# Copying out both upper parts of a PSUM bank before forming its two lower parts, in the second attention and in the stick-breaking mixer

## The chip, the cores and the metric

The kernel runs on one core of one Trainium2 chip. The metric is the device time of one execution in microseconds, taken as the median of several runs.

## The reference, cut to what matters

The program is a stack of two transformer-like blocks over 1024 tokens of width 1024, in f32: a differential attention and a multi-head latent attention (the first block), then a block with three mixers (spatial gating, stick-breaking, dilated window) and a gated feed-forward part. The change touches two places, the second attention and the stick-breaking mixer. In both a square of weights `p` (128 queries by up to 1024 keys) is multiplied with the values:

```python
# second attention (8 heads): all 1024 keys
p = jax.nn.softmax(sc, axis=-1)
return jnp.einsum('bhqk,bkhd->bqhd', p.astype(v.dtype), v)

# stick-breaking (6 heads): only the keys before the query
before = (k_pos[None, :] < q_pos[:, None])[None, None]
z = jnp.einsum('bqhd,bkhd->bhqk', q_blk, k).astype(jnp.float32) * scale
log_beta = jax.nn.log_sigmoid(z)
log_stay = jnp.where(before, jax.nn.log_sigmoid(-z), 0.0)
tail = lax.cumsum(log_stay, axis=3, reverse=True) - log_stay
weight = jnp.where(before, jnp.exp(log_beta + tail), 0.0)
return jnp.einsum('bhqk,bkhd->bqhd', weight.astype(v.dtype), v)
```

## The kernel before, in words

Nearly every product is made in three matmuls of a short f32 type (`fp32r`): each operand is split into an upper part (a cast, on ScalarE) and a lower part, which is the operand less its upper part (`lo`, a `tensor_sub`, by default on VectorE).

The program has four phases: the first attention (`layer0`, some 120 to 760 us in the trace), the second attention (`layer1`, its heads some 1050 to 1520 us), the mixers (the stick-breaking heads some 1790 to 2095 us) and the feed-forward part. The first attention's order on each engine is written out by hand in a table and pinned. In all other phases the order is not pinned: the functions are generators that are interleaved (`merge`, `pace`, `ahead`), and when the context is left a scheduler puts the instructions of each engine in order, by the program's order, by priorities (`tc.high_priority`) and by its own estimate of when each is ready; it also settles the buffers (`TileContext(nc, schedule_with_timeline_sim=True, auto_bufs=True)`). Each engine then runs its instructions strictly in that order.

In the second attention a tile is 128 queries of a head against 1024 keys. TensorE forms the scores (tile `s`), VectorE takes the row maximum, ScalarE the exponential (tile `e`), VectorE the reciprocal of the sum, GpSimd scales the row. Then `pt_fill` turns the row: four 128x128 transposes fill one PSUM bank (tile `m`, taken from `pm`), so that a tile has two banks. Each bank holds four key blocks, and is read out in two parts of two key blocks each (128x256): the upper part by ScalarE into one `pt` tile, the lower part by VectorE into the next. After four tiles `pv` multiplies `v` with the eight `pt` tiles. There are 8 heads of 8 tiles: 64 tiles and 128 banks.

In the stick-breaking mixer a tile has `qi + 1` key blocks, for `qi` from 0 to 7. A head then has 12 banks, of which 8 are read in two parts and 4 in one; six heads give 72 banks, 48 of them with two parts. The row passes VectorE (minimum), ScalarE (`Exp`, `Ln`), VectorE (a scan), ScalarE (`Exp`) and GpSimd (a product) before it is turned by the same `pt_fill`.

In the first attention the function `turns` of `da_tile` does the corresponding work, in PSUM tiles named `t`: there both upper parts are already copied first and the two lower parts are formed after them. The dilated-window mixer turns its rows with code of its own. Neither is touched.

A PSUM bank is one object to the framework's tracking of dependences: an instruction of one engine that reads a bank is made to wait for an earlier reader of the same bank on another engine.

Of the kernel before, what the change touches and what calls it, by code (L numbers as in the profile page):

```python
# [122 lines left out]
class Net:  # L123
# [689 lines left out]
    def pt_fill(self, pts, p, slot, ktiles):  # L813

        nc = self.nc
        qs = slice(slot * 128, slot * 128 + 128)
        for g in range((ktiles + 3) // 4):
            n = min(4, ktiles - 4 * g)
            ps = self.pm((128, 4, 128))
            for i in range(n):  # L820
                kt = 4 * g + i
                nc.tensor.transpose(ps[:, i], p[:, kt * 128:(kt + 1) * 128], self.ident)
            for i in range(0, n, 2):
                m = min(2, n - i)
                hi, lo = (pts[4 * g + i + x][:, 0:m, qs] for x in range(2))
                nc.scalar.copy(hi, ps[:, i:i + m])
                self.lo(lo, ps[:, i:i + m], hi)

    def pv(self, v, pts):

# [1330 lines left out]
```

## Time and profile before

| what | value |
|---|---|
| time, median of 3 runs | 2925.15 us (2916.08 to 2933.8) |
| the profiled execution's own time | 2909.92 us |
| its span | 2907.9 us |
| mean granted clock of TensorE | 0.956 |
| TensorE busy | 2629.5 us (90%) |
| VectorE busy | 2099.3 us (72%) |
| ScalarE busy | 1421.6 us (49%) |
| GpSimd busy | 1292.2 us (44%) |

The profile is that of one execution, which was a little faster than the median. Busy times are unions over the whole span; the stages differ, so that a change in one is to be read from that stage. In the views PE is TensorE's matmuls and PEld its weight loads, DVE is VectorE, ACT is ScalarE, POOL is GpSimd. All instructions of the kernel carry the line of one helper, so that groups are told apart by tile names.

### The profile page before, as it was taken

The numbers are of one execution on the slowest core, as the hardware profiler recorded it, in microseconds if no ns is written. First come the engines' busy times: TensorE is split into PE (matmuls) and PEld (weight loads), VectorE is DVE, ScalarE is ACT, GpSimd is POOL, SyncE is SP. The second block draws the span as 40 slices with busy tenths as digits, with TensorE's granted clock in tenths as the row PEclk, the third lists the DMA queues.
The fourth block names the chain that finished last, engine by engine and source line by source line (L and its number), as shares of the span: only waits on it lengthen the run. The fifth ranks groups of instructions, "written<-read, shape, count | busy, mean of one in ns | idle before, by whom it ended". The sixth has DMA issues, their size and how long they took to land. (4 is left out here: it accounts for less than half of the span.)

```text
span 2907.9 us, 34523 instructions
## 1 busy us (share of the span) xinstructions
PE 2629.5 (90%) x12023; PEld 2128.7 (73%) x12023; DVE 2099.3 (72%) x2696; ACT 1421.6 (49%) x2609; POOL 1292.2 (44%) x779
## 2 busy tenths in 40 slices
PE   7899999998899979999997798887978999997897
PEld 4678787887777867877775687776766777776676
DVE  7577877778642596667768563778768888899865
ACT  5455555556444534544554453667544344443432
POOL 2423323342344532212243332444447878778761
PEclk8999999999999999999998999999989999998998
DMA  7233333234541473223342356332621222234564
GB/s 292 66 97 101 109 109 105 66 95 141 174 131 42 127 254 106 71 89 118 117 132 80 80 82 112 91 87 85 197 89 51 88 79 73 87 124 146 187 237 147
DMA packets 308402, 338.91 MB, mean 117 GB/s; under 512 B 37428, under 2 KB 232068, under 8 KB 308228
## 3 DMA queue, kind: packets, MB, share of 16 engines
q1 hardware_dynamic: 308228, 336.69, 39.3%
q8 instruction: 96, 1.57, 0.2%
q14 instruction: 78, 0.64, 0.1%
HBM read 231.17 MB, written 60.89 MB: 100 GB/s over the span
## 5 line engine op out<-in xcount | busy, mean ns | idle before, releaser
L111 PE MATMUL m<-h,wh 128*128 128x512 f32 x3480 | 985.0, 402 | 48.1 <-DVE h L111 14.4
L111 PEld LDWEIGHTS m<-h,wh 128*128 128x128 f32 x3480 | 669.4, 194 | 204.2 <-DVE h L111 18.2
L111 POOL TENSOR_TENSOR wl<-wr,wh 128x1024 fp32r<-128x1024 f32 (+1 forms) x146 | 333.5, 2291 | 429.6 <-ACT wh L111 393.4
L111 PE MATMUL u<-h,wh 128*128 128x512 f32 x1264 | 408.3, 404 | 1.4 <-ACT h L111 0.8
L111 POOL TENSOR_SCALAR e<-e,cf 128x1024 f32<-128x1024 f32 x128 | 152.6, 1193 | 564.8 <-DVE cf L111 403.5
L111 PE MATMUL m<-h,wl 128*128 128x512 f32 x840 | 336.8, 402 | 7.8 <-POOL wl L111 7.8
L111 ACT ACTIVATE e<-s,cf 128x1024 f32<-128x1024 f32 x192 | 216.0, 1126 | 240.4 <-DVE cf L111 221.9
L111 ACT CAST wh<-wr 128x1024 fp32r<-128x1024 f32 (+3 forms) x252 | 202.6, 810 | 170.1 <-PE m L111 67.7
L111 DVE TENSOR_REDUCE cf<-s 128x1 f32<-128x1024 f32 x192 | 228.3, 1217 | 69.6 <-PE s L111 69.2
L111 PEld LDWEIGHTS u<-h,wh 128*128 128x128 f32 x1264 | 233.1, 191 | 47.5 <-ACT h L111 1.2
L111 PE MATMUL u<-h,wl 128*128 128x512 f32 x632 | 252.5, 400 | 12.7 <-POOL wl L111 12.7
L111 PE MATMUL s<-kk,qq 128*128 128x512 f32 (+3 forms) x752 | 187.3, 386 | 35.8 <-DVE e L111 18.7
L111 ACT CAST pt<-m 128x256 fp32r<-128x256 f32 (+2 forms) x396 | 140.1, 376 | 155.1 <-PE m L111 88.4
L111 PE MATMUL s<-h,wh 128*128 128x512 f32 x720 | 182.8, 399 | 35.5 <-DVE h L111 18.2
L111 PEld LDWEIGHTS m<-h,wl 128*128 128x128 f32 x840 | 164.1, 195 | 44.5 <-POOL wl L111 9.0
L111 DVE SCALAR_TENSOR_TENSOR e<-z,cf,e 128x1023 f32<-128x1023 f32 (+1 forms) x88 | 175.8, 2008 | 24.8 <-ACT e L111 24.6
L111 PE MATMUL s<-h,h 128*128 128x512 f32 x640 | 171.5, 414 | 20.8 <-DVE h L111 14.3
L111 PEld LDWEIGHTS s<-h,wh 128*128 128x128 f32 x720 | 136.5, 192 | 71.3 <-DVE h L111 19.7
L111 DVE TENSOR_TENSOR pt<-m,pt 128x256 fp32r<-128x256 f32 (+2 forms) x396 | 155.0, 416 | 41.6 <-ACT pt L111 34.6
L111 PEld LDWEIGHTS s<-kk,qq 128*128 128x128 f32 x752 | 135.9, 196 | 65.8 <-DVE e L111 20.4
L111 PE MATMUL m<-pt,v 128*128 128x512 f32 (+3 forms) x668 | 151.9, 371 | 17.1 <-ACT pt L111 8.6
L111 PEld LDWEIGHTS s<-h,h 128*128 128x128 f32 x640 | 122.3, 196 | 52.5 <-DVE h L111 17.8
(285 smaller groups left out, 4848.0 us busy)
## 6 DMA issues: line engine op xcount, KB each, us to landing
wr<-in_w_in_dram SPq DMA_DIRECT2D x61, 512.0 KB
wr<-in_w_out_dram SPq DMA_DIRECT2D x48, 512.0 KB
tb<-in_w_ada_dram SPq DMA_DIRECT2D x48, 512.0 KB
wr<-in_w_up_dram SPq DMA_DIRECT2D x47, 512.0 KB
qq<-ab SPq DMA_DIRECT2D x144, 128.0 KB
wr<-in_ada_w_dram SPq DMA_DIRECT2D x32, 512.0 KB
tf<-act SPq DMA_DIRECT2D x30, 512.0 KB
wr<-in_w_down_dram SPq DMA_DIRECT2D x30, 512.0 KB
```

What stands on the lines that cost most here:

```text
L111: ins = f(*args, **kw)
```

## The change

In `pt_fill` the loop over the two parts of a bank, which issued for each part the cast and then the subtraction, becomes two loops: first all casts of the bank, then all subtractions. Instructions, shapes and tiles stay the same. The function has two callers, `mla_attention` (second attention) and `mixer_b_attention` (stick-breaking).

```diff
@@ -820,11 +820,11 @@
             for i in range(n):
                 kt = 4 * g + i
                 nc.tensor.transpose(ps[:, i], p[:, kt * 128:(kt + 1) * 128], self.ident)
-            for i in range(0, n, 2):
-                m = min(2, n - i)
-                hi, lo = (pts[4 * g + i + x][:, 0:m, qs] for x in range(2))
-                nc.scalar.copy(hi, ps[:, i:i + m])
-                self.lo(lo, ps[:, i:i + m], hi)
+            parts = [(pts[4 * g + i], pts[4 * g + i + 1], i, min(2, n - i)) for i in range(0, n, 2)]
+            for hi, _, i, m in parts:
+                nc.scalar.copy(hi[:, 0:m, qs], ps[:, i:i + m])
+            for hi, lo, i, m in parts:
+                self.lo(lo[:, 0:m, qs], ps[:, i:i + m], hi[:, 0:m, qs])
```

## Rows read from the trace of the kernel before

**Rows 1.** The page: span, and busy time and share of each engine.
```profile
span 2907.9 us, 34523 instructions
...
PE 2629.5 (90%) x12023; PEld 2128.7 (73%) x12023; DVE 2099.3 (72%) x2696; ACT 1421.6 (49%) x2609; POOL 1292.2 (44%) x779
```

**Rows 2.** Busy time by stage: first attention, second attention, stick-breaking.
```profile
core 0: us, PE busy (x) PEld busy (x) DVE busy (x) ACT busy (x) POOL busy (x), PEclk, DMA share, GB/s
120.00:760.00 640.00, 611.61 (x2914) 497.07 (x2913) 506.88 (x717) 361.73 (x728) 214.62 (x118) 0.98 0.36 101
1050.00:1520.00 470.00, 443.06 (x2176) 364.26 (x2175) 327.62 (x618) 236.77 (x521) 121.23 (x102) 0.96 0.38 114
1790.00:2095.00 305.00, 260.47 (x1300) 216.33 (x1299) 228.25 (x318) 183.85 (x365) 130.15 (x76) 0.94 0.41 108
```

**Rows 3.** Groups by shape, whole span: busy us, mean ns; idle before, releasers.
```profile
L111 ACT CAST pt<-m 128x256 fp32r<-128x256 f32 x356 | 126.3, 374 | 146.5 <-PE m L111 80.1 <-DVE pt L111 61.1 <-issue 3.1
...
L111 DVE TENSOR_TENSOR pt<-m,pt 128x256 fp32r<-128x256 f32 x356 | 139.2, 415 | 35.1 <-ACT pt L111 31.5
L111 DVE TENSOR_TENSOR pt<-t,pt 128x256 fp32r<-128x256 f32 x256 | 95.8, 416 | 84.1 <-ACT pt L111 78.3 <-DMA qq<-ab 5.6
```

**Rows 4.** Timeline of ScalarE, one tile of the second attention.
```profile
1261.79 0.36 ACT L111 CAST pt<-m 128x256 fp32r<-128x256 f32 x1
1262.65 0.65 ACT L111 CAST pt<-m 128x256 fp32r<-128x256 f32 x2 [0.49 <-DVE pt L111]
...
1265.30 0.37 ACT L111 CAST pt<-m 128x256 fp32r<-128x256 f32 x1 [1.24 <-DVE pt L111]
```

**Rows 5.** Timeline of VectorE, the same tile.
```profile
1262.19 0.42 DVE L111 TENSOR_TENSOR pt<-m,pt 128x256 fp32r<-128x256 f32 x1
1263.12 0.42 DVE L111 TENSOR_TENSOR pt<-m,pt 128x256 fp32r<-128x256 f32 x1 [0.51 <-ACT pt L111]
1263.71 1.23 DVE L111 TENSOR_REDUCE cf<-s 128x1 f32<-128x1024 f32 x1 [0.16 <-PE s L111]
1264.86 0.41 DVE L111 TENSOR_TENSOR pt<-m,pt 128x256 fp32r<-128x256 f32 x1
...
1265.71 0.42 DVE L111 TENSOR_TENSOR pt<-m,pt 128x256 fp32r<-128x256 f32 x1 [0.38 <-ACT pt L111]
```

**Rows 6.** Timeline of one bank in the first attention.
```profile
404.63 0.65 ACT L111 CAST pt<-t 128x256 fp32r<-128x256 f32 x2 [4.90 <-PE t L111]
...
405.68 0.76 DVE L111 TENSOR_TENSOR pt<-t,pt 128x256 fp32r<-128x256 f32 x2 [5.56 <-DMA qq<-ab]
```

**Rows 7.** TensorE's waits, second attention: waited for; us, times, longest.
```profile
PE s L111 <- DVE h L111: 8.5, 3, 3.5
...
PE m L111 <- DVE v L111: 3.4, 1, 3.4
PE m L111 <- DVE t L111: 3.1, 2, 1.7
...
PE m L111 <- DVE cf L111: 2.4, 3, 1.2
PE m L111 <- DVE pt L111: 1.3, 2, 0.8
```

**Rows 8.** TensorE's waits, stick-breaking.
```profile
PE s L111 <- DVE e L111: 18.7, 13, 6.4
...
PE m L111 <- DVE pt L111: 4.5, 6, 1.6
PE m L111 <- DVE h L111: 3.0, 1, 3.0
...
PE m L111 <- ACT pt L111: 1.8, 3, 1.0
```

**Rows 9.** VectorE's subtractions by shape, second attention, then stick-breaking.
```profile
L111 DVE TENSOR_TENSOR pt<-m,pt 128x256 fp32r<-128x256 f32 x256 | 100.7, 417 | 29.4 <-ACT pt L111 26.0
...
L111 DVE TENSOR_TENSOR pt<-m,pt 128x256 fp32r<-128x256 f32 x97 | 37.3, 409 | 5.7 <-ACT pt L111 5.5
```

## The prediction

> **What bounds the kernel now.** I read the page first: TensorE is busy 90% of the span and nothing else is above 73% [rows 1]. That is an average, so I cut it into the stages where `pt_fill` runs. In the second attention TensorE is busy 443.06 of 470 us, which leaves 26.9 us idle; VectorE has 327.62 us of work there (70%), ScalarE 236.77 (50%). In the stick-breaking stretch TensorE is busy 260.47 of 305 us, 44.5 us idle, and VectorE 228.25 (75%) [rows 2]. So TensorE sets the pace in both, loosely in the second, and a change that gives it no work and takes none away can only act on these 71.4 us of idle time, or add to them.
>
> The third view, the groups by shape, says whether the order that the change removes costs anything at all. Before a cast out of an `m` bank ScalarE sat idle 61.1 us in total until a VectorE subtraction had ended; VectorE before its subtractions sat idle 31.5 us until a cast had ended [rows 3]. The timeline of one tile shows how: the second cast of a bank begins 0.04 us after the first subtraction has ended (1262.19 + 0.42 = 1262.61, then 1262.65). The same happens in the other bank, but there the first subtraction stands behind a 1.23 us row maximum on VectorE and ends at 1265.27, so the last cast starts only at 1265.30, after 1.24 us of idle time on ScalarE [rows 4, 5]. A part that lies ready in PSUM waits for a subtraction of another part.
>
> The fourth view, who TensorE waits for, says whether that reaches the bound. In the second attention only 1.3 us of its waits, twice, end on a subtraction into `pt`; in stick-breaking 4.5 us in six, and 1.8 us in three on a cast into `pt` [rows 7, 8]. Together 7.6 us: the big idle times on ScalarE lie almost wholly beside TensorE work.
>
> **The change part by part.** Nothing is added or dropped: no DMA, no matmul, no tile; 128 banks of the second attention and 48 of stick-breaking have two parts, 176 in all, and only they change. (24 more stick-breaking banks have one part, which stay as they are.) What is left out is the alternation: three handovers between engines in a bank become one.
>
> *One bank by itself.* Before, with nothing else in the queues: 0.36 + 0.42 + 0.37 + 0.42 with three handovers of 0.04 makes 1.69 us. After: two casts back to back took 0.65, one handover 0.04, two subtractions back to back 0.76 [rows 4 to 6], in sum 1.45 us. So a bank is free 0.24 us earlier, and its first lower part comes 0.29 us later (0.69 after the start in place of 0.40). Where another instruction slips in between the two subtractions, as the 1.23 us row maximum can, a bank gains over 1 us: in the tile shown, from the first cast to the last subtraction, 1261.79 to 1266.13, it is 4.34 us, and four casts and four subtractions without gaps would need about half of that.
>
> *On the engines.* ScalarE can lose most of its 61.1 us of waits; at 50% it is no bound, and what it does next is mostly waiting for something else anyway, so I cost this gain at nothing. Its cover is the TensorE work of other tiles and of the next head; without that cover it would be worth at most the 7.6 us above. VectorE saves about 0.08 us where two subtractions newly stand together (0.42 + 0.42 against 0.76), at most 176 x 0.08 = 14 us over 775 us of which it is idle 219: nothing on the path.
>
> *The one wait that grows.* The first subtraction needs only its own cast, but will now wait for both. The trace shows this where the order is already so: in the first attention two casts run from 404.63 to 405.28 and the pair of subtractions begins at 405.68 [rows 6]. Behind the waiting subtraction stand, in VectorE's queue, row maxima, scans, the minimum that frees a score bank, and the lower parts of the next head's keys; TensorE waits for those (`h`, `v`, `t`, `e` in [rows 7, 8]). Bounds for VectorE's new idle time: from below, one chance to wait in place of two, half of today's 31.5 us gone, about -16 us; from above, the rate of the first attention, 78.3 us over 128 banks, 0.61 us each, against 0.20 in the second attention (26.0 over 128) and 0.11 in stick-breaking (5.5 over 48) [rows 3, 9], which makes (0.61 - 0.20) x 128 = 52 us and (0.61 - 0.11) x 48 = 24 us more. I take the lower end's direction, since the casts that were held back 61.1 us will now run early and VectorE finds them done more often; the first attention's order was pinned by hand and is a farther row.
>
> The rows above show a second cast that waits although it reads other columns of the bank than the subtraction does [rows 4, 5]. The Trainium skill (PSUM — Partial Sum Buffer, section on PSUM bank collisions) says why: no two of TensorE, ScalarE and VectorE may be in one bank and quadrant at once, even reading disjoint columns, so such accesses have to be kept apart by semaphores. That rule speaks against the change as well: the first subtraction can't start beside the second cast. If a subtraction needed its own cast alone, each bank would gain 0.29 us on its first lower part; neither the sum nor the range uses this.
>
> *The order of everything else.* These two phases are not pinned. The scheduler sees 176 banks with other dependences and may place fills, weight casts and row maxima elsewhere in 775 us. No row prices that. It can't win more than the 71.4 us of TensorE's idle time in both stages [rows 2]; I take 0 with a quarter of it, 18 us, on either side.
>
> **The sum.** Second attention, half of 1.3: -0.6 us. Stick-breaking, about half of 4.5 + 1.8: -3.0. VectorE's 16 us fewer idle us reach TensorE in the share in which it waits for VectorE at all, 18.7 of 470 and some 26 of 305 us [rows 7, 8], 4% to 9%: -1.0. Reordering: 0. In all -4.6 us on the profiled execution's 2909.92 us (span 2907.9, so 2 us lie around it): 2905.3. That execution stands 15.2 us under the median of the runs shown, so against the median 2925.15 - 4.6 = 2920.5. Changes below 0.5%, 14.6 us, can't be told from none in this kernel, whose own three runs lie 17.7 us apart.
>
> **Rivals.**
>
> *Faster: banks and VectorE's queue free up for others.* The `m` banks are shared by projections, transposes and `pv`; freed earlier, and with lower parts of keys and values less late, half of all TensorE waits that end on VectorE vanish: (18.7 + 26.2) / 2 = 22 us, 2902.7 us. For it: the longest of these waits are 3.4 to 6.4 us, as long as a whole tile's read-out. Against it: only 5.8 of those 44.9 us name `pt` [rows 7, 8].
>
> *Slower: the head of VectorE's queue.* The first subtraction, now behind two casts, holds up VectorE at the first attention's rate. In the second attention VectorE has 142 us of slack, so that 52 us more hide; in stick-breaking it already is what TensorE waits for most (18.7 us in 13 waits on the minimum that frees a score bank), and 24 us could come through in full: 2925.15 + 24 = 2949. It decides against the change from about 60% of that price on (14.6 of 24). For it: 78.3 us of such waits in the first attention. Against it: ScalarE is at 60% in this stretch, so two casts seldom stand behind much.
>
> *Nothing changes:* the scheduler already finds other banks' work for the gaps, and rows 4 show a pair of casts, of two banks, without a gap. Then 2925. Against a total blank: the 61.1 us of waits are real, so that the order must change somewhere.
>
> *The new order is worse or better by itself,* 2907 or 2943, by the quarter above.
>
> **How the numbers follow.** Forecast (a few us, with small reordering) 0.46; faster rival 0.23; slower rival 0.14; nothing 0.06; a new order worse by itself 0.05, better by itself 0.06. Faster by over 0.5% (under 2910.5): the faster rival nearly whole, the better order in half, a little of the forecast: 0.27. Slower (over 2939.8): most of the slower rival, the worse order: 0.18. Between: 0.55. The forecast's own range is 2909 to 2932, the sum with the spread of three runs. The range that should hold 8 in 10 reaches past the faster rival and most of the way to the slower one: 2897 to 2944.
>
> **What would show it.** In the changed kernel's groups by shape: still 356 casts and 356 subtractions of 128x256; the casts' idle time ended by a subtraction falls from 61.1 us to under 10; casts stand in pairs of 0.65 us and subtractions in pairs of 0.76 in the timeline; the subtractions' busy union falls from 139.2 to about 127 us. VectorE's idle time before them until a cast stays under 31.5 us if I am right, and goes above 70 us if the slower rival is. TensorE's idle time stays within a few us of 26.9 and 44.5. I would be wrong if it moves by more than 15 us in either stage, or if stages that the change doesn't touch move as well, which would be the scheduler's doing.

## The result, and the profile after

The changed kernel takes 2899.61 us (median of 9 runs, 2892.39 to 2903.0) against 2922.85 us before (median of 9 on the same chips, 2906.94 to 2933.8): a ratio of 0.9926, 95% interval 0.9903 to 0.9948. That is faster by 0.74%, some 22 us. It lies in the stated range (2897 to 2944), 2.6 us above its lower end, and not in the case that the forecast held likeliest.

The page of the changed kernel, span and busy time by engine:

```profile
span 2890.7 us, 34687 instructions
...
PE 2617.9 (91%) x12023; PEld 2121.8 (73%) x12023; DVE 2090.2 (72%) x2696; ACT 1415.2 (49%) x2609; POOL 1297.0 (45%) x779
```

The span fell by 17.2 us, TensorE's busy time by 11.6 us with the same 12023 matmuls, so that the rest, 5.6 us, is idle time in sum over the whole kernel [rows 1]. The stages say more (changed kernel; first attention, second attention, stick-breaking, the last two with their ends shifted):

```profile
120.00:760.00 640.00, 611.37 (x2901) 497.20 (x2900) 504.30 (x717) 360.37 (x726) 213.27 (x119) 0.98 0.36 101
1050.00:1500.00 450.00, 437.17 (x2192) 359.71 (x2193) 320.21 (x620) 231.74 (x523) 129.37 (x104) 0.99 0.41 122
1770.00:2076.00 306.00, 256.58 (x1313) 214.88 (x1312) 230.28 (x317) 183.33 (x366) 128.20 (x76) 0.94 0.42 108
```

The first attention is what it was. In the second attention TensorE's idle time is 12.8 us in 450 in place of 26.9 in 470, and the granted clock is 0.99 in place of 0.96; in stick-breaking it is 49.4 us in place of 44.5 [rows 2]. Measured from the start of the first score matmul to that of the last matmul of `pv`, the second attention's heads take 426.4 us in place of 450.9: 24.5 us, more than the 17.2 us between the two spans. The stick-breaking stretch, from the start of its first scan to that of its last `pv` matmul, takes 262.5 in place of 262.9. The other 7 us went the other way in parts that the change doesn't touch: the second attention's first score matmul comes 3.7 us later, and of 20.3 us of lead when the last part of the feed-forward phase begins 17.2 are left at its end.

The groups of the read-out in the changed kernel, by shape:

```profile
L111 ACT CAST pt<-m 128x256 fp32r<-128x256 f32 x356 | 113.0, 385 | 109.0 <-PE m L111 102.9 <-issue 3.1 <-POOL e L111 1.1
...
L111 DVE TENSOR_TENSOR pt<-m,pt 128x256 fp32r<-128x256 f32 x356 | 130.9, 413 | 30.8 <-ACT pt L111 30.5
```

The 61.1 us in which ScalarE waited for a subtraction are gone from the row. VectorE's wait for casts is 30.5 us after 31.5: it neither halved nor grew to the first attention's rate [rows 3]. And TensorE's waits, first in the second attention (1062 to 1478 us), then in stick-breaking (1770 to 2076 us), changed kernel:

```profile
PE m L111 <- DVE pt L111: 3.8, 5, 1.5
PE m L111 <- DVE v L111: 0.4, 1, 0.4
PE m L111 <- DVE t L111: 0.2, 1, 0.2
```

```profile
PE s L111 <- DVE e L111: 11.1, 8, 6.3
PE m L111 <- DVE t L111: 7.5, 2, 6.8
...
PE m L111 <- DVE pt L111: 7.4, 5, 6.4
PE m L111 <- ACT pt L111: 3.7, 5, 1.9
```

In the second attention the waits for `h` (8.5 us) are gone, those for `v` and `t` nearly so; those that name `pt` rose, from 1.3 to 3.8 us [rows 7]. In stick-breaking one wait shrank and others took its place [rows 8].

**Where the 24.5 us were.** Before, TensorE runs dry at every second change of head. This is VectorE's timeline of the kernel before at such a place, and under it TensorE's:

```profile
1237.16 1.28 DVE L111 SCALAR_TENSOR_TENSOR z<-tb,cf,z 128x1024 f32<-128x1024 f32 x1 [0.31 <-DVE t L111]
1238.36 0.42 DVE L111 TENSOR_TENSOR pt<-m,pt 128x256 fp32r<-128x256 f32 x1
1238.70 1.28 DVE L111 SCALAR_TENSOR_TENSOR z<-tb,cf,z 128x1024 f32<-128x1024 f32 x1
1239.89 0.69 DVE L111 TENSOR_TENSOR h<-m,h 128x512 fp32r<-128x512 f32 x1
1240.49 1.08 DVE L111 TENSOR_TENSOR pt<-m,pt 128x256 fp32r<-128x256 f32 x3
```

```profile
1237.00 0.63 PE L111 MATMUL m<-cr,e 128*128 128x128 f32 x4 [1.66 <-DVE t L111]
1237.38 0.71 PE L111 MATMUL s<-h,h 128*128 128x512 f32 x2
1240.63 1.65 PE L111 MATMUL s<-h,h 128*128 128x512 f32 x3 [2.54 <-DVE h L111]
```

The 1.28 us rows `z<-tb` are weight chunks of the third block's modulations: filling work without any haste, one after another on VectorE. One stands between two subtractions, and behind it stands `h`, the lower part of the next head's keys, for which TensorE waits 2.54 us, having waited 1.66 us for `t` before. The changed kernel at the corresponding change of head, same two engines:

```profile
1231.33 0.75 DVE L111 TENSOR_TENSOR pt<-m,pt 128x256 fp32r<-128x256 f32 x2
1231.99 1.28 DVE L111 SCALAR_TENSOR_TENSOR z<-tb,cf,z 128x1024 f32<-128x1024 f32 x1
1233.18 0.75 DVE L111 TENSOR_TENSOR pt<-m,pt 128x256 fp32r<-128x256 f32 x2
1233.85 0.68 DVE L111 TENSOR_TENSOR h<-m,h 128x512 fp32r<-128x512 f32 x1
```

```profile
1231.56 1.29 PE L111 MATMUL m<-cr,e 128*128 128x128 f32 x8
1232.60 0.71 PE L111 MATMUL s<-h,h 128*128 128x512 f32 x2
1234.08 0.70 PE L111 MATMUL m<-qq,wh 128*128 128x512 f32 x2 [0.76 <-DVE pt L111]
```

The chunks are still there, between pairs of subtractions; by the time of `h` four subtractions are done, where it was one, the next eight transposes are in, and TensorE waits 0.76 us in all.

The bubble costs twice. Two pairs of heads of the kernel before, and a piece just behind the bubble shown (columns as in the stages above; the last but two is the granted clock):

```profile
1121.98:1175.85 53.87, 49.95 (x252) 41.22 (x251) 39.03 (x77) 24.93 (x59) 11.40 (x11) 0.97 0.42 126
1175.85:1223.07 47.22, 47.16 (x244) 39.17 (x243) 28.18 (x64) 24.75 (x59) 11.41 (x11) 1.00 0.20 55
1223.07:1278.18 55.11, 50.91 (x252) 41.91 (x251) 38.83 (x75) 24.93 (x59) 11.42 (x11) 0.94 0.41 123
1278.18:1325.43 47.25, 47.19 (x244) 39.17 (x243) 28.19 (x64) 24.75 (x59) 11.43 (x11) 1.00 0.22 62
...
1239.00:1246.00 7.00, 5.37 (x15) 4.30 (x16) 6.38 (x11) 1.95 (x6) 0.00 (x0) 0.53 0.83 294
```

and the same two pairs in the changed kernel:

```profile
1122.46:1168.51 46.05, 45.31 (x231) 36.92 (x230) 35.15 (x70) 20.76 (x51) 10.81 (x10) 1.00 0.48 143
1168.51:1219.15 50.64, 50.52 (x265) 42.14 (x264) 30.73 (x71) 27.43 (x67) 12.61 (x12) 1.00 0.20 56
1219.15:1265.43 46.28, 45.35 (x231) 36.82 (x230) 34.94 (x68) 20.83 (x52) 10.83 (x10) 1.00 0.48 142
1265.43:1316.07 50.64, 50.52 (x265) 42.14 (x264) 30.73 (x71) 27.44 (x67) 12.61 (x12) 1.00 0.22 62
```

A pair is 496 matmuls in either kernel. Idle time falls from 3.98 to 0.86 and from 4.26 to 1.05 us, 6.3 us in both pairs; busy time falls from 97.11 to 95.83 and from 98.10 to 95.87, 3.5 us, because behind each bubble TensorE ran at the lower of its two clock levels (0.53 granted over 1239 to 1246, that is nearly all at 1.2 GHz). So in these two pairs about two thirds of the gain is the waiting and one third the clock. In the record of the granted clock the kernel before has 23.9 us at half clock at four places: three changes of head, and a wait of 3.4 us for `v` in the last head. The changed kernel has none from 1062.4 to 1478.8 us. The Trainium skill (TensorE: Matmul & The Clock Gate, section on HAM oscillation) describes a kernel whose TensorE is throttled by its waits for DMA data and does the next work cold; the trace agrees, with waits for VectorE in place of a DMA, here 4.2 us of them around 1.1 us of work.

That chunks stood there can be read from the program's order on VectorE. Of the second attention's 128 banks:

```
                         banks  subtractions adjacent  a weight chunk between  a score row maximum between
kernel before              128                      9                      21                           18
changed kernel             128                    127                       0                            0
```

Before, the second subtraction could not be ready until a cast had run that itself waited for the first; the scheduler put something else there (that it did so because the place was free is a reading and not shown). After it, the two are ready together. In stick-breaking VectorE's order shows 32 of 48 banks with a scan or a score row's minimum between the two subtractions before, and none after; what that was worth, the runs on either place say.

### The profile page after: what moved, and what is told of

The parts are those of the page before. It is cut to its first block, busy times and chain, and to the rows that moved or that the text cites. A ratio compares the mean times of both kernels' runs of the same rounds, so it can differ in the third digit from the quotient of the medians.

```text
span 2890.7 us, 34687 instructions
## 1 busy us (share of the span) xinstructions
PE 2617.9 (91%) x12023; PEld 2121.8 (73%) x12023; DVE 2090.2 (72%) x2696; ACT 1415.2 (49%) x2609; POOL 1297.0 (45%) x779
## 5 line engine op out<-in xcount | busy, mean ns | idle before, releaser
L111 PE MATMUL u<-h,wl 128*128 128x512 f32 x632 | 252.2, 399 | 12.8 <-POOL wl L111 12.8
L111 PE MATMUL s<-h,wh 128*128 128x512 f32 x720 | 183.9, 401 | 35.8 <-DVE h L111 17.1
L111 ACT CAST pt<-m 128x256 fp32r<-128x256 f32 (+2 forms) x396 | 126.4, 387 | 117.8 <-PE m L111 111.6
L111 DVE TENSOR_TENSOR pt<-m,pt 128x256 fp32r<-128x256 f32 (+2 forms) x396 | 146.3, 415 | 37.0 <-ACT pt L111 36.4
L111 PE MATMUL m<-pt,v 128*128 128x512 f32 (+3 forms) x668 | 145.8, 363 | 22.7 <-ACT pt L111 13.0
L111 DVE TENSOR_TENSOR pt<-t,pt 128x256 fp32r<-128x256 f32 x256 | 95.7, 415 | 86.7 <-ACT pt L111 80.4
```

What stands on the lines that cost most here:

```text
L111: ins = f(*args, **kw)
```

## The experiments

The theory (A): the gain lies in the second attention; a chunk or another long row gets between the subtractions of a bank, what is urgent on VectorE comes late at changes of head, TensorE runs dry and its clock falls. The rivals: (B) each saved handover or pairing gives a few tenths of a microsecond in every bank; (C) longer holding of banks would hurt; (L) it was a lucky order of the scheduler; (D) any extra work on the read-out's engines costs alike. Twelve kernels ran. Each ratio is to runs of the kernel before on the same chip. The stretch is that from the first score matmul of the second attention to its last `pv` matmul; the last column is the time at half clock in it, of which 13.7 us lie in the first head of both kernels.

| kernel | time us | ratio to before (95%) | stretch us | half clock us |
|---|---|---|---|---|
| before | 2922.85 | 1 | 450.9 | 37.5 |
| changed | 2899.61 | 0.9926 (0.9903 to 0.9948) | 426.4 | 13.7 |
| casts first in second attention only | 2896.48 | 0.9918 (0.9898 to 0.9939) | 427.6 | 13.7 |
| casts first in stick-breaking only | 2926.21 | 1.0007 (0.9995 to 1.0019) | 451.4 | 41.0 |
| casts first over a whole tile | 2902.35 | 0.993 (0.9909 to 0.9951) | 425.9 | 17.1 |
| a bank for each part, old order | 2940.98 | 1.0067 (1.005 to 1.0085) | 465.3 | 34.1 |
| chunks left out, old order | 2886.24 | 0.9859 (0.9826 to 0.9891) | 413.8 | 6.8 |
| chunks left out, new order | 2879.57 | 0.984 (0.9817 to 0.9863) | 409.3 | 3.4 |
| lead 32, old order | 2917.82 | 0.998 (0.9965 to 0.9995) | 446.0 | 27.3 |
| lead 32, new order | 2899.51 | 0.9908 (0.9885 to 0.9931) | 426.9 | 13.7 |
| chunks elsewhere, old order | 2916.91 | 0.998 (0.9966 to 0.9994) | 437.1 | 26.5 |
| chunks elsewhere, new order | 2909.69 | 0.9951 (0.9934 to 0.9968) | 431.4 | 16.7 |
| lead 48, old order | 2925.42 | 0.9999 (0.9987 to 1.001) | 445.6 | 27.3 |
| lead 48, new order | 2893.99 | 0.9898 (0.9882 to 0.9915) | 425.1 | 13.7 |

**Which of the two places.** The new order in one caller, the old one in the other:

```diff
-                self.pt_fill(pts, e, slot, 8)
+                self.pt_fill(pts, e, slot, 8, True)         # second attention
-                    self.pt_fill(pts, u, slot, qi + 1)
+                    self.pt_fill(pts, u, slot, qi + 1, False)   # stick-breaking
```

> Casts first in the second attention alone, the old alternation in stick-breaking. Theory A (the gain is the second attention's: at every second change of head VectorE put a weight chunk between the subtractions of one bank, TensorE ran dry for 2 to 4 us, and its granted clock fell to half for 3 to 7 us behind it): the whole gain, 20 to 26 us under the kernel before, TensorE idle in the second attention near 13 us in place of 27, and no stretch at half clock between its first and last heads. Theory B (the gain comes from both places, a few tenths of a microsecond per bank): 128 of 176 banks, about 17 us of the 23 seen.

Then the reverse, `False` and `True`:

> Casts first in stick-breaking alone. Theory A: no gain, within 3 us of the kernel before, and the drops to half clock in the second attention all there. Theory B: 48 of 176 banks, about 6 us faster.

All of the gain is the second attention's: 0.9918 of the time before, 24 us, with its stretch at 427.6 us, and nothing for stick-breaking, whose interval excludes the 6 us of theory B. Theory A holds in both, down to the clock. The 32 stick-breaking banks that lost the long rows between their subtractions gained nothing that could be measured by it.

**One step further.**

```diff
         for g in range((ktiles + 3) // 4):
...
-            for hi, _, i, m in parts:
-                nc.scalar.copy(hi[:, 0:m, qs], ps[:, i:i + m])
...
+            parts += [(pts[4 * g + i], pts[4 * g + i + 1], ps, i, min(2, n - i)) for i in range(0, n, 2)]
+        for hi, _, ps, i, m in parts:
+            nc.scalar.copy(hi[:, 0:m, qs], ps[:, i:i + m])
+        for hi, lo, ps, i, m in parts:
+            self.lo(lo[:, 0:m, qs], ps[:, i:i + m], hi[:, 0:m, qs])
```

> One step further than the change: both banks of a tile are turned, then all four casts, then all four subtractions, in both places. Theory A (what counts is that a cast never waits for a subtraction, and the changed kernel has that already): the changed kernel's time within 6 us, ScalarE's wait for subtractions near zero in both. Theory B (each handover between the engines that is saved gives time): a further handover saved per tile of 64, some 5 to 9 us faster than the changed kernel. Theory C (banks held longer hurt): slower than the changed kernel by 5 us or more, with TensorE waiting for banks.

2902.35 us, within 3 us of the changed kernel (by the ratios within 1 us, with intervals of some 6 us to either side): one more handover per tile is worth nothing that can be measured (against B), and neither does a bank held a little longer cost anything that can be (against C).

**The wait taken away in another way.**

```diff
-            ps = self.pm((128, 4, 128))
+            pss = [self.pm((128, 4, 128)) for _ in range(0, n, 2)]
...
-                nc.tensor.transpose(ps[:, i], p[:, kt * 128:(kt + 1) * 128], self.ident)
+                nc.tensor.transpose(pss[i // 2][:, i % 2], p[:, kt * 128:(kt + 1) * 128], self.ident)
...
-                nc.scalar.copy(hi, ps[:, i:i + m])
-                self.lo(lo, ps[:, i:i + m], hi)
+                nc.scalar.copy(hi, pss[i // 2][:, 0:m])
+                self.lo(lo, pss[i // 2][:, 0:m], hi)
```

> The old order of issue, cast and subtraction part by part, but each part of two key blocks has a PSUM bank of its own (four banks a tile in place of two), so that no cast stands behind a subtraction of the same bank. Theory A (the wait for the subtraction of the same bank is the cost): ScalarE's 61 us of waits for subtractions go, and most of the gain is seen, 10 to 23 us under the kernel before, unless the four m banks run short, which would show as TensorE waiting on pt before transposes. Theory B (the gain is the pairing of casts and of subtractions, back to back): no gain, 2915 to 2930 us.

It is slower by 0.67%, which neither theory gave as its main case. Its groups by shape, and TensorE's longest waits in the second attention:

```profile
L111 ACT CAST pt<-m 128x256 fp32r<-128x256 f32 x356 | 115.4, 381 | 148.7 <-PE m L111 139.9 <-DVE e L111 4.6 <-issue 2.9
```

```profile
PE m L111 <- DVE pt L111: 10.5, 10, 1.6
PE s L111 <- ACT e L111: 6.2, 3, 3.6
PE s L111 <- DVE pt L111: 5.1, 3, 1.9
```

ScalarE's waits for subtractions are gone as in the changed kernel, and the casts' busy union is 115.4 us, so that they now run in pairs. Still TensorE waits 15.6 us for `pt`, where it was 1.3 us before, and the half clock is there as in the kernel before. Twice as many banks now come out of the same four. So to take away the ScalarE waits that the row before showed so plainly is not by itself enough for the gain; which of the two, shortage of banks or old order, weighs how much in this run can't be told, as the edit changes both.

**The chunks.** Seven of the eight chunks of each modulation are left out, with the old and with the new order:

```diff
             for k in range(8):
+                if k > 0:
+                    if k < 7:
+                        yield
+                    continue
                 wt = self.load(w_tag, [128, 1024])
```

> The kernel before, with 7 of the 8 weight chunks of each modulation left out (loads and VectorE work of 42 of 48 chunks; the modulations of the third block are then not the reference's). Theory A (the bubbles at every second change of head come from weight chunks of 1.3 us on VectorE that get in between the subtractions of a bank): in the second attention no wait of TensorE over 1 us at the changes of head after the first, no stretch at half clock there, and the heads of the second attention within 6 us of the same kernel with casts first. Theory B (the alternation costs by itself, chunks or not): bubbles and half clock stay, and the stretch of the second attention's heads is 15 us or more longer than in the kernel with casts first.

> The changed kernel, with the same 42 of 48 weight chunks left out. Theory A: within 6 us of the run above in the second attention; theory B: 15 us or more faster than it. Either way no half clock between the second and the last head, as in the changed kernel.

The busy time from 1045 to 1400 us, old order, and who TensorE waited for there:

```profile
1045.00:1400.00 355.00, 350.53 (x1821) 291.56 (x1821) 226.04 (x506) 190.20 (x443) 90.57 (x83) 1.00 0.25 70
```

```profile
PE m L111 <- DVE v L111: 3.4, 1, 3.4
PE s L111 <- ACT e L111: 0.6, 1, 0.6
PE m L111 <- ACT e L111: 0.4, 1, 0.4
```

With the alternation untouched, but without chunks, TensorE waits 4.4 us in 355, at full clock. From the first score matmul of the first head to that of the last head the old order takes 330.2 us and the new one 330.8. The whole difference of 4.5 us between the stretches comes in the last head, where the one wait for `v` of 3.4 us stands, with 3.4 us at half clock behind it. That wait is not at a change of head; at those theory A holds, and B falls. In this kernel's order on VectorE, 18 of the 128 banks still have a row maximum of 1.2 us between their two subtractions, as before, and the chunks are gone from there: so it is the chunks that made the alternation dear. All in all the difference between the orders shrinks from 24.5 to 4.5 us. Leaving the chunks out takes their load off VectorE as well as their place; the changed kernel, with every chunk still on VectorE, is the one that moves the place alone.

**The same chunks on other engines,** in a complete kernel, by a switch that it has: scaled on ScalarE, added up on GpSimd.

```diff
-MSH = ()
+MSH = (1, 2, 3, 4, 5, 6, 7)
```

> The kernel before, complete, but 7 of the 8 chunks of each modulation of the third block are scaled on ScalarE (about 1.1 us each) and added up on GpSimd in place of the 1.3 us on VectorE. Theory A (a chunk on VectorE between the subtractions of a bank is what costs): bubbles and half clock at the changes of head go although the read-out still alternates; heads of the second attention within 8 us of the run below, total 2893 to 2908 us. Theory D (any extra work in the read-out's two engines costs the same): the chunks now hold up casts on ScalarE, bubbles stay, 2915 us or more.

> The changed kernel with the same chunks on ScalarE and GpSimd. Theory A: no faster than the changed kernel by more than 6 us, since its bubbles were gone already: 2893 to 2905 us. Theory D: casts held up by chunks, slower than the changed kernel by 5 us or more.

Half a hit for each theory. The two orders differ by 5.7 us in the stretch, as A said (under 8), and between the first scores of the fourth and of the eighth head both take 190.2 us. But both totals miss A's figures, half clock stays around the first two changes of head in the old order, and the new order is slower than the changed kernel, which D had foreseen (by the ratios some 7 us, with intervals that just overlap). ScalarE's waits in the old order, 1040 to 1480 us:

```profile
ACT tb L111 <- DMA tb<-in_w_ada_dram: 29.5, 18, 4.7
ACT pt L111 <- DVE pt L111: 24.2, 41, 2.1
```

A chunk whose load hasn't landed now stands at the head of ScalarE's queue, with casts and exponentials behind it; the longest wait of TensorE, 8.4 us at the second head, was for a cast of `h`. The head of a queue is the same trap on another engine.

**Luck of the scheduler.** The second attention's lead of priority, which has nothing to do with the read-out, at 32 and at 48 in place of 40, for both orders:

```diff
-HP_M = 40
+HP_M = 32
```

> The kernel before with the second attention's lead of priority set from 40 to 32, which has nothing to do with the read-out of a bank but gives the scheduler another order. Theory A (casts first is the cause): 2912 to 2935 us, with bubbles at changes of head. Theory L (any new order might have won, this one was luck): could come out near 2900 as well.

> The changed kernel with the second attention's lead of priority set from 40 to 32. Theory A: stays at 2890 to 2908 us without bubbles. Theory L: may fall back to 2915 or more.

> The kernel before with the second attention's lead of priority at 48 in place of 40, a third order of the scheduler with the old read-out. Theory A: 2912 to 2930 us, half clock at changes of head again. Theory L: near 2900 could come out.

> The changed kernel with the lead at 48. Theory A: 2890 to 2908 us, no half clock after the first head. Theory L: 2915 or more could come out.

Old order: 2922.85, 2917.82, 2925.42. New order: 2899.61, 2899.51, 2893.99. The groups don't meet; the medians of one order spread by about 4 us to either side, and each pair differs by 18 us or more. Theory L falls. One thing is not as A had it: the lead of 32 with the new order has a wait of 2.8 us for `h` at the second head, though without half clock behind it. The lead of 48 with the new order is the fastest complete kernel that ran, by its ratio 0.9898; against the changed kernel on the same chip it wasn't timed, and the intervals of the two ratios overlap.

## Why the prediction was right in range and wrong in its main case

*The bound and the waits* were read rightly: TensorE sets the pace, the waits between ScalarE and VectorE are real, 61.1 us went to nothing, casts run in pairs. The subtractions' busy union came to 130.9 us (127 forecast).

*The step that failed* is the one that cost ScalarE's saved waits "at nothing", covered by "the TensorE work of other tiles and of the next head", and bounded without that cover by 7.6 us, the waits that name `pt`. The cover is missing at a change of head, where the next scores need `h` from VectorE's queue, in which the chunks stood between the subtractions. The waits for `h`, `v` and `t` were in rows 7, 15.0 us of them; they were taken up in the sum only by a share (4% to 9%, -1.0 us), as though a wait on VectorE were spread evenly. They vanished nearly whole, to 0.6 us. The right bound was all of TensorE's waits that end on VectorE in that stage, 18.7 us (4.4 after), and the clock on top. The prediction's own sign of being wrong, TensorE's idle time in a stage moving by more than 15 us, just did not show: it fell from 26.9 to 12.8 us.

*The clock* was not in the sum at all. The rows showed 0.96 in that stage, against 0.98 in the first attention; about a third of what was won in the two pairs of heads is there.

*Stick-breaking,* forecast -3.0, gave nothing: 1.0007 when changed alone. Its waits for `pt` rose rather than fell.

*VectorE's wait for casts:* forecast halved, measured 30.5 against 31.5. The slower rival, which needed over 70 us, falls with it, and with it the weight given to the rule on banks as an argument against the change: in none of the second attention's 128 banks does the changed kernel begin a subtraction before both casts have ended, and VectorE's waits before subtractions have not grown by it. (Rows 6, which the prediction took as showing this wait, do not: they put the 5.56 us before that pair down to a DMA.)

*The faster rival* came in. The range holds the result only because it was made to reach past this rival. Its time (2902.7 us) was 3 us off, and its mechanism, the lower parts of keys and values less late, is what the timelines show. Its place was half wrong: it took half of the VectorE waits in both stages, while most in one and none in the other went, and the clock made up the rest; that the sums meet so closely is luck. (Its 26.2 us for stick-breaking leave out two small waits; the view has 27.7.) It had been given a chance of 0.23 on the ground that few of those waits name `pt`; that was the misreading, since a releaser's name says who came last and not who stood before it in the queue.

*The new order of everything else* was taken as 0 with 18 us to either side. For an order that the read-out has no part in, three settings of the lead put it at about 4. But the gain itself came by this way, the chunks being put elsewhere on VectorE (21 of 128 banks before, none after): the term was taken as though it had no direction, and the change gave it one.

## What to carry to other kernels

When two in-order engines read one bank in turn, issue all of one engine's reads before the other's: the saved handovers are small, but a pair of instructions that become ready together gives a scheduler no hole to fill with long work that isn't urgent. Not every hole costs: here it did where the next head's keys stood behind it, while in stick-breaking holes with scans and minima in them were closed without a gain that could be measured (1.0007). Judge a wait by what stands behind it in its queue, not by the name of the tile that it releases, and look at the places where the cover of other work ends (here a change of head) rather than at the average. A bubble of a few microseconds on TensorE is to be priced with the half clock that follows it.

## What the hardware showed that was not expected

In the kernel before, TensorE's granted clock fell to half for 3.4 us at waits of 1.4 and 2.5 us, for 6.8 us at waits of 1.7 and 2.5 us, and for 6.8 us at each of two single waits of 3.5 and 3.4 us, in stretches where it is otherwise full. The length of a wait doesn't settle it: a single wait of 2.8 us (lead 32, new order) and one of 1.5 us (changed kernel) brought no fall, while one of 1.2 us in the kernel with casts first over a whole tile had 3.4 us at half clock behind it. And taking the wait between the two readers away by a bank for each part was dearer than the wait: 1.0067 of the time, with 15.6 us of TensorE waits for `pt` in the second attention.
